# Attention units of a head pair alternate, queries lie by token half, logits are requested by chunks, and inverse row sums are stored as columns

## The chip, the cores and the metric

The kernel runs on one core of one Trainium2 chip. The metric is device time of one execution in microseconds (us); lower is better. Five engines work side by side, each through its own instructions in a fixed order: PE (matrix multiply; its weight loads, "PEld", overlap its matmuls), DVE (vector), ACT (scalar functions), POOL (general, also issues DMAs) and SP (issues most DMAs). Engines wait for each other through semaphores. PE writes to PSUM, of which the kernel uses eight banks of 128 partitions by 512 float32; SBUF holds the operands.

## What is computed

One layer of a decoder for 1024 tokens of width 1024:

```python
h = x @ w_in                       # columns: pool u | q | k | v | forget logits
pool_out = scale * GroupLinear(trailing_mean_w(u) - u)         # w = 2, 4, 8, 16
# attention, 8 heads of 64, causal:
s = q @ k.T * HEAD_DIM**-0.5 + c[t] - c[s]                     # c = cumsum(log sigmoid(f))
attn = softmax(where(s_pos <= t_pos, s, -1e30)) @ v
x = layer_norm(alpha * x + concat(pool_out, attn) @ w_out)
x = layer_norm(alpha * x + relu(x @ w_mlp1)**2 @ w_mlp2)
```

Everything is float32. The kernel splits each operand in a high and a low part and makes three matmuls of one product (`three`, lines 80 to 84).

## The kernel before

The program runs in stages, all of which keep PE busy: values and forget gates and three of the four pool groups (up to about 105 us of the profiled span), attention with the output projection beginning under its end (105 to 345), the rest of the output projection, the first layer norm and both MLP products (a fast 2x2 block scheme), to the end.

**Attention units.** The eight heads form four pairs p = 0 to 3; e = 0, 1 is the head in its pair. A unit (p, e, m) has 256 queries, two tiles of 128 (i = 2m and 2m+1), and the keys up to them, so m = 3 is the heaviest unit and m = 0 the lightest. Line 703 lists the units of pairs 0 to 2 with one head after the other, each falling through m = 3, 2, 1, 0; line 704 lists the last pair with m rising and e inside.

**A unit's two halves.** `att_probs` asks PE for the logits of one query tile in chunks of up to 512 keys (L375, into one of three "s" banks). DVE adds the gate row and finds the running minimum of the negated logits (L380). After the last chunk ACT takes the exponential and its row sum (L382). `att_values` transposes the probabilities on PE (L405, into one of two "pt" banks), splits them (ACT L406, DVE L407) and multiplies with V (L420, into the single "pv" bank); ACT and DVE evacuate that bank (L429, L430) before the next unit's product may begin. `att_values` of one unit runs the generator `att_probs` of the next unit (`ahead`) between its steps: one `yield` per query tile, the first at its first step, the rest at step min(m, (m+1)//2+1).

**Fill.** Between those steps `fillstep` takes pieces of other PE work, three matmuls each: the q and k projection of the next pair (`qk_proj`, L82 to L84 into "mm" banks) in pairs 0 to 2, and in the last pair the last pool group and the output projection of the first two token tiles (`last_fill`). What remains of a projection is run when a pair ends (line 728).

**Row sums.** A head's inverse row sums come from DVE (L443) as columns: [128 tokens, 8 tiles]. `row_scales` turns them on PE (L466, into a "pt" bank), copies them out on ACT into the one buffer `row` (L468) and stores [8, 128] rows to DRAM (`rin_dram`, L469), once per head in pairs 0 to 2 and once per unit in the last pair: 14 times. They are read back, broadcast over partitions, by `attention_part` (L580), which scales the attention output by them (L584) and splits it for the output projection. For the first token tiles the last pair's heads are read by the call named `late` (lines 529 and 544).

**Buffers.** Tags share slots: "A" has 9 (probabilities, their transposes, gate rows), "Q" has 10 (k, q, sums of the pool groups). A gate row of a head (L351) is held from just before its first unit to its last.

**What sets the order.** Each engine's order is fixed at build time by a scheduler that goes through the program's instructions by priority and readiness as it estimates them; on the chip every engine goes through its list in that order, and waits where an operand is late.

Of the kernel before, what the change touches and what calls it, by code (L numbers as in the profile page):

```python
# [14 lines left out]
P = 128  # L15
S = 1024
D = 1024
NT = S // P
# [3 lines left out]
NPAIR = NH // 2  # L22
# [3 lines left out]
CH = 512  # L26
NCH = S // CH
# [9 lines left out]
def trunk(ctx, tc, xT, xn, wuqk, wvf, bf, poolw, pscale, wout, g1, b1, w1, w2, g2, b2, out):  # L37
# [5 lines left out]
    nc = tc.nc  # L43
# [268 lines left out]
    def qk_proj(p, tag=None):  # L312
        if p < NPAIR - 1:
            KS, Q1, Q2 = zip(*([slot("Q", [S]) for _ in range(3)] for _ in range(2)))
            q = {(i, e, c): (Q1, Q2)[i][e][:, c * CH : (c + 1) * CH] for i in range(2) for e in range(2) for c in range(NCH)}
        else:
            KS = [slot("Q", [S]) for _ in range(2)]
            both = {(i, c): slot("Q", [2, CH]) for c in range(NCH) for i in range(2)}
            q = {(i, e, c): both[i, c][:, e] for i in range(2) for e in range(2) for c in range(NCH)}
# [14 lines left out]
        for c in (0, 1) if p == NPAIR - 1 else (1, 0):  # L334
# [18 lines left out]
    def att_probs(p, e, m, prob):  # L353
# [3 lines left out]
        h = 2 * p + e  # L357
# [3 lines left out]
        for i in (2 * m + 1, 2 * m) if falling else (2 * m, 2 * m + 1):  # L361
# [7 lines left out]
            for a in range(0, nk, CH):  # L369
# [11 lines left out]
                top = nm  # L381
            nc.scalar.activation(pt[:, :nk], pt[:, :nk], AF.Exp, bias=nm, scale=-1.0, accum_out=rsum[h][:, i : i + 1])  # L382
            yield

    def att_values(p, e, m, prob, ahead):
# [24 lines left out]
        def multiply(jp, tt):  # L410
# [13 lines left out]
            if jp == m:  # L424
# [10 lines left out]
                if last:  # L435
                    row_scales(h, 2 * m, 2)
                elif m == 0:
                    row_scales(h, 0, NT)

        if p == NPAIR - 1 or m == 0:  # L440
            ri = small([P, NT], "ri", bufs=3)
            i, n = (2 * m, 2) if p == NPAIR - 1 else (0, NT)
            nc.vector.reciprocal(ri[:, :n], rsum[h][:, i : i + n])  # L443
            inverse[h, i] = ri

        for jp in range(m + 1):
            left.append((multiply, jp, turned(jp)))
            if jp == 0:
                fill["last"] = fill["sub"]
                next(ahead, None)  # L450
            if jp == min(m, (m + 1) // 2 + 1):
                run(ahead)
# [3 lines left out]
    left, inverse = [], {}  # L456
# [5 lines left out]

    def row_scales(h, i, n):
        ri = inverse.pop((h, i))
        tp = bank("pt")
        nc.tensor.transpose(tp[0:n, 0:P], ri[:, :n], ident)  # L466
        row = small([NT, P], "row")
        nc.scalar.copy(row[0:n], tp[0:n, 0:P])  # L468
        nc.sync.dma_start(rin_dram[h, i * P : (i + n) * P].rearrange("(i q) -> i q", q=P), row[0:n])  # L469
# [233 lines left out]
    order = [(p, e, m) for p in range(NPAIR - 1) for e in range(2) for m in (3, 2, 1, 0)]  # L703
# [631 lines left out]
```

## Time and profile before

| | |
|---|---|
| median of 3 runs | 1028.21 us (1027.87 to 1028.32) |
| the profiled execution | 1028.26 us, its span 1026.5 us |
| granted PE clock over the span | 0.997 |
| PE busy | 1013.1 us, 99% |
| DVE, ACT, POOL busy | 754.4 us, 513.3 us, 153.6 us |

A span is the time from the first to the last instruction of the program; 1.8 us of the execution lie around it. Matmuls overlap in the profile: one of 512 columns is shown with 0.39 us, but the next may start 0.23 us after it. So "PE busy 99%" hides short waits, and starts that are further apart than usual show them. In "engine line waited for" rows the numbers are the sum in us, the times, and the longest.

### The profile page before, as it was taken

To read this page: it belongs to the slowest core of one execution; us is meant where nothing else is said; L and a number is where in the kernel's file an instruction comes from. 1 tells how busy PE (TensorE), PEld (TensorE's weight loads), DVE (VectorE), ACT (ScalarE), POOL (GpSimd) and SP (SyncE) were. 2 spreads that over 40 slices of the span, in tenths; PEclk is the share of its full clock that TensorE was granted. 3 is DMA by queue.
4 is the path that set the end of the run, shared out by engine and by line. 5 is a ranking of instruction groups with operands and counts; after the bars stand their busy time and mean duration, and the time that the engine had idled before them with its cause. 6 is when DMAs were issued, how large, how long until landed. Compare 5 with 4: busy or idle time off the path is not lost.

```text
span 1026.5 us, 14095 instructions
## 1 busy us (share of the span) xinstructions
PE 1013.1 (99%) x4976; PEld 843.8 (82%) x4976; DVE 754.4 (73%) x1303; ACT 513.3 (50%) x825; POOL 153.6 (15%) x269
## 2 busy tenths in 40 slices
PE   9999999999999999999999999999999999999996
PEld 9988888888788888888888888888888888888884
DVE  6576677777868798989888787798866565565547
ACT  5423665666755333678667667669521121221152
POOL 0200111111110032112221221220000000000057
PEclk9999999999999999999999999999999999999998
DMA  9702211111682633259676675665999888878753
GB/s 354 285 28 88 97 52 53 34 48 52 205 290 91 188 141 103 82 185 362 235 273 236 241 275 222 251 260 191 350 309 289 298 265 264 289 237 274 231 179 123
DMA packets 113399, 206.17 MB, mean 201 GB/s; under 512 B 9576, under 2 KB 77608, under 8 KB 113328
## 3 DMA queue, kind: packets, MB, share of 16 engines
q1 hardware_dynamic: 94176, 136.97, 40.7%
q0 software_dynamic: 18720, 67.64, 17.0%
q8 instruction: 39, 0.64, 0.2%
q10 hardware_dynamic: 432, 0.66, 0.2%
q14 instruction: 32, 0.26, 0.1%
HBM read 132.29 MB, written 72.94 MB: 200 GB/s over the span
## 4 chain that ended last, share of the span: by engine, by line
PE 58%; DVE 2%; issue 0%; ACT 0%; DVEq 0%
PE s L1136 17%; PE s L796 11%; PE pv L1136 9%; PE mm L796 7%; PE pt L796 7%; PE pv L796 4%; PE pt L1136 2%; PE mm L1136 2%; DVE B L71 0%; DVE bns L639 0%; DVE A L664 0%; DVE pt L661 0%; DVE pt L1153 0%; DVE A L870 0%; DVE pv L1153 0%
## 5 line engine op out<-in xcount | busy, mean ns | idle before, releaser
L71 ACT CAST B<-S 128x1024 fp32r<-128x1024 f32 (+1 forms) x78 | 67.6, 880 | 162.9 <-DMA S<-in_w_dram 85.0
L796 PE MATMUL s<-B,Q 128*128 128x512 f32 x492 | 116.4, 389 | 0.2 <-ACT B L71 0.2
L796 PEld LDWEIGHTS s<-B,Q 128*128 128x128 f32 x492 | 92.3, 188 | 19.7 <-ACT B L71 0.6
L71 DVE TENSOR_TENSOR B<-S,B 128x1024 fp32r<-128x1024 f32 (+1 forms) x78 | 78.0, 1008 | 37.7 <-ACT B L71 37.6
L1136 PE MATMUL s<-B,Q 128*128 128x512 f32 x402 | 98.5, 390 | 0.0
L1136 PEld LDWEIGHTS s<-B,Q 128*128 128x128 f32 x402 | 75.5, 188 | 16.5
L71 ACT CAST Q<-S 128x1024 fp32r<-128x1024 f32 (+2 forms) x54 | 55.7, 1031 | 63.6 <-PE s L796 17.0
L921 POOL DMA_DIRECT2D hid_dram<-A x90 | 48.1, 538 | 218.1 <-ACT A L918 171.5
L1136 PE MATMUL s<-B,A 128*128 128x512 f32 x321 | 80.3, 394 | 0.0
L71 DVE TENSOR_TENSOR Q<-S,Q 128x1024 fp32r<-128x1024 f32 (+2 forms) x54 | 65.5, 1213 | 12.8 <-ACT Q L71 12.6
L796 PE MATMUL pt<-B,Q 128*128 128x512 f32 x312 | 74.6, 389 | 0.0
L1136 PEld LDWEIGHTS s<-B,A 128*128 128x128 f32 x321 | 60.4, 188 | 13.9
L796 PE MATMUL mm<-B,Q 128*128 128x512 f32 x300 | 71.6, 389 | 0.0
L382 ACT ACTIVATE A<-A,nm 128x1024 f32<-128x1024 f32 (+7 forms) x64 | 49.7, 777 | 42.0 <-DVE nm L380 41.9
L407 DVE TENSOR_TENSOR A<-pt,A 128x512 fp32r<-128x512 f32 (+1 forms) x80 | 50.1, 633 | 25.1 <-ACT A L406 24.3
L796 PEld LDWEIGHTS pt<-B,Q 128*128 128x128 f32 x312 | 58.5, 188 | 12.1
L796 PEld LDWEIGHTS mm<-B,Q 128*128 128x128 f32 x300 | 56.3, 188 | 11.7
L919 DVE TENSOR_TENSOR A<-A,A 128x1024 f32<-128x1024 f32 x45 | 53.6, 1218 | 0.0
L406 ACT CAST A<-pt 128x512 fp32r<-128x512 f32 (+1 forms) x80 | 42.4, 541 | 22.2 <-PE pt L405 21.6
L375 PE MATMUL s<-Q,Q 128*128 128x512 f32 (+2 forms) x192 | 52.2, 368 | 1.3 <-DVE nm L380 1.3
L420 PE MATMUL pv<-A,B 128*128 128x256 f32 x320 | 53.1, 289 | 0.2 <-DVE U L430 0.2
L420 PEld LDWEIGHTS pv<-A,B 128*128 128x128 f32 x320 | 45.8, 189 | 6.4 <-DVE U L430 3.2
(432 smaller groups left out, 2290.1 us busy)
## 6 DMA issues: line engine op xcount, KB each, us to landing
hid_dram<-A POOLq DMA_DIRECT2D x105, 512.0 KB, 3.8
S<-in_w_dram SPq DMA_DIRECT2D x62, 512.0 KB, 4.4
Q<-hid_dram SPq DMA_DIRECT2D x98, 256.0 KB, 5.3
A<-hid_dram SPq DMA_DIRECT2D x82, 256.0 KB, 5.3
S<-in_wuqk_dram SPq DMA_DIRECT2D x12, 512.0 KB, 4.7
wo_dram<-Q POOLq DMA_DIRECT2D x10, 512.0 KB, 4.3
B<-wo_dram SPq DMA_DIRECT2D x10, 512.0 KB, 6.8
Q<-hid_dram SPq DMA_DIRECT2D x39, 128.0 KB, 3.2
```

The lines of the kernel that those rows point to most:

```text
L71: return nc.scalar.copy(hi, src).ins, nc.vector.tensor_tensor(lo, src, hi.bitcast(F32), ALU.subtract).ins
L375: nc.tensor.matmul(sp, rows, KS[:, a:b], start=n == 0, stop=n == 1 and not diag)
L382: nc.scalar.activation(pt[:, :nk], pt[:, :nk], AF.Exp, bias=nm, scale=-1.0, accum_out=rsum[h][:, i : i + 1])
L406: nc.scalar.copy(tt[:, 0, ev], tp[:, ev])
L407: fill["sub"] = nc.vector.tensor_tensor(tt[:, 1, ev], tp[:, ev], tt[:, 0, ev].bitcast(F32), ALU.subtract).ins
L420: nc.tensor.matmul(ov, V[j][:, h].rearrange("p s d -> p (s d)"), tt[:, s, a:b], start=(j == 0 and s == 0), stop=(j == 2 * m + 1 and s == 1),)
L796: nc.tensor.matmul(dst, b[x][:, k], A[a][y][:, k], start=first and k == 0 and i == 0, stop=k == H - 1 and i == 2, skip_group_check=not first,)
L919: nc.vector.tensor_tensor(x, x, hi.bitcast(F32), ALU.subtract)
L921: nc.gpsimd.dma_start(hid_dram[self.u, :, i, AT[name] : AT[name] + 2 * CH], part.rearrange("p q n t -> p (q n t)"))
L1136: nc.tensor.matmul(dst, h[:, p_], w[q_], start=first and u == self.us[0] and j == 0, stop=u == self.us[-1] and j == 2, skip_group_check=no ...
```

## The change

- Pairs 0 to 2 list their units with the two heads alternating: (3, e=0), (3, e=1), (2, e=0) and so on. The last pair's list is as it was.
- `qk_proj` allocates q of every pair by token half, both heads in one slot, as the last pair did already; six slots for a pair as before. Pairs 0 to 2 make the second token half first.
- `att_probs` yields after each chunk of logits, not only after a query tile, and `att_values` asks for one piece at each of its steps but the last, and for the rest at the last.
- `row_scales` is gone. The inverse row sums are stored as the columns they are, straight from DVE's output, by one DMA when a head's (or last pair's unit's) probabilities are done: [128, 8] or [128, 2] single elements of 4 bytes to places of stride 1 over the partitions. This stands at the start of `att_values` and no longer behind its last multiply.

```diff
     def qk_proj(p, tag=None):
-        if p < NPAIR - 1:
-            KS, Q1, Q2 = zip(*([slot("Q", [S]) for _ in range(3)] for _ in range(2)))
-            q = {(i, e, c): (Q1, Q2)[i][e][:, c * CH : (c + 1) * CH] for i in range(2) for e in range(2) for c in range(NCH)}
-        else:
-            KS = [slot("Q", [S]) for _ in range(2)]
-            both = {(i, c): slot("Q", [2, CH]) for c in range(NCH) for i in range(2)}
-            q = {(i, e, c): both[i, c][:, e] for i in range(2) for e in range(2) for c in range(NCH)}
+        halves = (0, 1) if p == NPAIR - 1 else (1, 0)
+        KS = [slot("Q", [S]) for _ in range(2)]
+        both = {(i, c): slot("Q", [2, CH]) for c in halves for i in range(2)}
+        q = {(i, e, c): both[i, c][:, e] for i in range(2) for e in range(2) for c in range(NCH)}
...
                 top = nm
+                if b < nk:
+                    yield
             nc.scalar.activation(pt[:, :nk], pt[:, :nk], AF.Exp, bias=nm, scale=-1.0, accum_out=rsum[h][:, i : i + 1])
...
-                if last:
-                    row_scales(h, 2 * m, 2)
-                elif m == 0:
-                    row_scales(h, 0, NT)
 
         if p == NPAIR - 1 or m == 0:
-            ri = small([P, NT], "ri", bufs=3)
             i, n = (2 * m, 2) if p == NPAIR - 1 else (0, NT)
+            ri = small([P, NT], "ri", bufs=4)
             nc.vector.reciprocal(ri[:, :n], rsum[h][:, i : i + n])
-            inverse[h, i] = ri
+            nc.sync.dma_start(rin_dram[h, i * P : (i + n) * P].rearrange("(i q) -> q i", q=P), ri[:, :n])
 
         for jp in range(m + 1):
             left.append((multiply, jp, turned(jp)))
             if jp == 0:
                 fill["last"] = fill["sub"]
+            if jp < m:
                 next(ahead, None)
-            if jp == min(m, (m + 1) // 2 + 1):
+            else:
                 run(ahead)
...
-    order = [(p, e, m) for p in range(NPAIR - 1) for e in range(2) for m in (3, 2, 1, 0)]
+    order = [(p, e, m) for p in range(NPAIR - 1) for m in (3, 2, 1, 0) for e in range(2)]
     order += [(NPAIR - 1, e, m) for m in range(4) for e in range(2)]
```

How the order of the engines changes, at three places. A row names the line, the operation, out<-in and the shape.

**PE, the heaviest unit (m = 3) of the second head of pair 1.** Q_1201 (before) and Q_1202 (changed) hold its k as s<-Q; mm is fill. Before:

```order
L375 MATMUL s_2058<-Q_1201,Q_1202 128x512
L375 MATMUL s_2058<-Q_1201,Q_1203 128x512
L375 MATMUL s_2063<-Q_1201,Q_1202 128x512
L375 MATMUL s_2063<-Q_1201,Q_1203 128x512
L375 MATMUL s_2071<-Q_1201,Q_1202 128x512
L375 MATMUL s_2071<-Q_1201,Q_1203 128x512
L82 MATMUL mm_2042<-B_390,B_2039 128x512
L83 MATMUL mm_2042<-B_390,B_2039 128x512
L84 MATMUL mm_2042<-B_390,B_2039 128x512
L420 MATMUL pv_1216<-A_1984,B_417 128x256
L375 MATMUL s_2076<-Q_1201,Q_1202 128x384
L375 MATMUL s_2076<-Q_1201,Q_1203 128x384
```

Changed (L372 is what L375 was):

```order
L372 MATMUL s_1809<-Q_1202,Q_1203 128x512
L372 MATMUL s_1809<-Q_1202,Q_1204 128x512
L83 MATMUL mm_1744<-B_172,B_1741 128x512
L372 MATMUL s_1833<-Q_1202,Q_1203 128x512
L372 MATMUL s_1833<-Q_1202,Q_1204 128x512
L84 MATMUL mm_1744<-B_172,B_1741 128x512
L82 MATMUL mm_1744<-B_172,B_1741 128x512
L372 MATMUL s_1860<-Q_1202,Q_1203 128x512
L372 MATMUL s_1860<-Q_1202,Q_1204 128x512
L83 MATMUL mm_1744<-B_172,B_1741 128x512
L84 MATMUL mm_1744<-B_172,B_1741 128x512
L82 MATMUL mm_1744<-B_187,B_1741 128x512
```

Three banks were filled in one go and the fourth chunk followed four matmuls later; now the chunks stand apart, and the fourth one (not shown) comes after two groups of transposes. The first unit of pairs 1 and 2 still asks for three banks in one go.

**PE, unit (0, 0, 2), from the last logits to its transposes.** Before, from its last logits on (s_1282):

```order
L375 MATMUL s_1282<-Q_975,Q_977 128x256
L82 MATMUL mm_1209<-B_172,B_1206 128x512
L405 MATMUL pt_1252<-ident_63,A_1152 128x128
L405 MATMUL pt_1252<-ident_63,A_1139 128x128
L405 MATMUL pt_1252<-ident_63,A_1152 128x128
L405 MATMUL pt_1252<-ident_63,A_1139 128x128
L420 MATMUL pv_1216<-A_1218,B_417 128x256 x4
L83 MATMUL mm_1209<-B_172,B_1206 128x512
L405 MATMUL pt_1267<-ident_63,A_1139 128x128
L405 MATMUL pt_1267<-ident_63,A_1152 128x128
L405 MATMUL pt_1267<-ident_63,A_1139 128x128
L84 MATMUL mm_1209<-B_172,B_1206 128x512
```

Changed, the same (last logits s_1386, first transpose pt_1405):

```order
L372 MATMUL s_1386<-Q_975,Q_978 128x256
L82 MATMUL mm_1323<-B_397,B_1209 128x512
L83 MATMUL mm_1323<-B_397,B_1209 128x512
L84 MATMUL mm_1323<-B_397,B_1209 128x512
L419 MATMUL pv_1219<-A_1332,B_430 128x256 x4
L82 MATMUL mm_1323<-B_404,B_1209 128x512
L83 MATMUL mm_1323<-B_404,B_1209 128x512
L84 MATMUL mm_1323<-B_404,B_1209 128x512
L82 MATMUL mm_1323<-B_404,B_1209 128x512
L83 MATMUL mm_1323<-B_404,B_1209 128x512
L84 MATMUL mm_1323<-B_404,B_1209 128x512
L404 MATMUL pt_1405<-ident_63,A_1365 128x128
```

Before, eleven more rows stand between the last one shown and the unit's own transposes; now these come at the end of the piece.

**SP, in the last pair, up to the loads that `attention_part` makes for the first three pairs (S<-mix, S<-rin).** Before:

```order
L432 DMA mix_dram<-U_3041 64x256
L561 DMA B_3215<-wo_dram 128x1024
L469 DMA rin_dram<-row_3120 8x128
L561 DMA B_3216<-wo_dram 128x1024
L432 DMA mix_dram<-U_3114 64x256
L561 DMA B_3215<-wo_dram 128x1024
L469 DMA rin_dram<-row_3164 2x128
L577 DMA S_3183<-mix_dram 128x768
L580 DMA S_3184<-rin_dram 64x3x256 x2
```

Changed:

```order
L439 DMA rin_dram<-ri_2986 128x2x1
L549 DMA B_3048<-wo_dram 128x1024
L431 DMA mix_dram<-U_3023 64x256
L549 DMA B_3184<-wo_dram 128x1024
L439 DMA rin_dram<-ri_3060 128x2x1
L549 DMA B_3185<-wo_dram 128x1024
L431 DMA mix_dram<-U_3097 64x256
L439 DMA rin_dram<-ri_3104 128x2x1
L549 DMA B_3184<-wo_dram 128x1024
L565 DMA S_3157<-mix_dram 128x768
L568 DMA S_3158<-rin_dram 64x3x256 x2
```

The store of head 5 (128x8x1) has moved further up, ahead of the first of these wo loads, and three stores of the last pair's units stand before the loads where one row store stood. From the second part of the output projection on (the last 1010 rows of PE) every engine's order is what it was, but for buffer numbers.

More of the change, by code (lines that the diff above doesn't have):

```diff
@@ L333, in qk_proj @@
         sc = HD ** -0.5
-        for c in (0, 1) if p == NPAIR - 1 else (1, 0):
+        for c in halves:
             qp = bank(tag)
@@ L454, in att_values @@
             values(2)
-    left, inverse = [], {}
+    left = []
     def values(n):
@@ L461, in values @@
             step(jp, tt)
[L463 to L469, printed above, removed]
     g0 = qk_proj(0)
```

## The prediction

> **What bounds the kernel now.** I read the page first, then the chain of work that ended last, then a table of windows by stage, then what PE's weight loads waited for between 105 and 345 us, then the timeline at single waits. Page, part 1 and the chain by engine:
>
> ```profile
> PE 1013.1 (99%) x4976; PEld 843.8 (82%) x4976; DVE 754.4 (73%) x1303; ACT 513.3 (50%) x825; POOL 153.6 (15%) x269
> PE 58%; DVE 2%; issue 0%; ACT 0%; DVEq 0%
> ```
>
> PE is the bound, and the chain names almost nothing else. The windows (us, then busy time of PE, PEld, DVE, ACT, POOL with counts, PE's granted clock, DMA share, GB/s):
>
> ```profile
> 105.00:262.00 157.00, 155.61 (x912) 130.73 (x911) 117.72 (x290) 101.81 (x217) 26.58 (x72) 1.00 0.18 56
> 262.00:345.00 83.00, 82.23 (x461) 66.77 (x459) 61.32 (x140) 48.15 (x99) 8.50 (x18) 1.00 0.62 198
> 345.00:1014.00 669.00, 668.82 (x2958) 550.18 (x2957) 500.26 (x715) 317.90 (x429) 104.24 (x139) 1.00 0.69 238
> ```
>
> From 345 us on PE idles for 0.2 of 669 us and its order is unchanged, so what attention gains or loses arrives at the end at full value. The granted clock is 1.00 in all three, so no term comes from it. In attention the 2.2 us that PE shows as idle are not all that it loses, because a matmul is drawn longer than the distance to the next start. The weight loads show the waits better (sum in us, times, longest):
>
> ```profile
> PEld s L375 <- DVE nm L380: 4.6, 10, 0.9
> PEld pv L420 <- DVE U L430: 3.2, 10, 0.6
> PEld pt L405 <- ACT A L382: 2.5, 9, 0.4
> PEld pt L405 <- ACT row L468: 2.3, 6, 0.6
> ...
> PEld pt L466 <- DVE A L407: 1.4, 6, 0.2
> ```
>
> Logits wait for a free "s" bank, values for the "pv" bank's evacuation, transposes for the exponential or for the row sums' copy. These five rows hold 14.0 us, of which PE feels a part. With the turned sums' own time this bounds the gain.
>
> **Term 1, row sums leave PE: -1.5 us.** Fourteen transposes and fourteen ACT copies go:
>
> ```profile
> L466 PE MATMUL pt<-ident,ri 128*2 128x128 f32 (+1 forms) x14 | 3.8, 272 | 0.0
> ```
>
> What one takes is its share of the starts, not 272 ns. In the timeline (start, length):
>
> ```profile
> 188.11 0.39 PE L83 MATMUL mm<-B,B 128*128 128x512 f32 x1
> 188.34 0.39 PE L84 MATMUL mm<-B,B 128*128 128x512 f32 x1
> ```
>
> and at a transpose of row sums
>
> ```profile
> 317.09 0.40 PE L84 MATMUL mm<-B,Q 128*128 128x512 f32 x1
> 317.40 0.27 PE L466 MATMUL pt<-ident,ri 128*2 128x128 f32 x1
> 317.42 0.71 PE L375 MATMUL s<-Q,Q 128*128 128x512 f32 x2
> 318.13 0.55 PE L405 MATMUL pt<-ident,A 128*128 128x128 f32 x3
> ```
>
> Full matmuls start 0.23 apart. From 317.09 to 317.42 it is 0.33 with the transpose between, so 0.10 to 0.11 each, and 14 x 0.11 = 1.5 us. The bound above is the 3.8 us of the group. The copies were off the path in themselves: ACT is busy 150 of 240 us here. What takes their place is one DMA issue on SP, of which more below, and the reciprocal, which DVE makes before and after.
>
> **Term 2, waits for the row copy: -1.1 us.** The one buffer `row` is not what PE waits for; the "pt" bank that holds the turned sums is, until ACT has copied it. Where it shows:
>
> ```profile
> 223.07 0.49 PE L375 MATMUL s<-Q,Q 128*128 128x512 f32 x1
> 223.70 0.44 PE L405 MATMUL pt<-ident,A 128*128 128x128 f32 x2
> ```
>
> ```profile
> 275.47 0.33 PE L375 MATMUL s<-Q,Q 128*128 128x384 f32 x1
> 276.07 0.66 PE L405 MATMUL pt<-ident,A 128*128 128x128 f32 x4 [0.27 <-ACT row L468]
> ```
>
> 0.63 - 0.23 = 0.40; 0.60 - 0.17 (three quarters of 0.23 for 384 columns) = 0.43; at 317.42, 0.71 - 0.46 = 0.25: 1.1 us. The other three of the six I take as hidden. Between nothing, if the transposes would have waited for something else at the same moment, and 2.3 + 1.4 = 3.7, all that the two weight-side rows hold, I take what is seen.
>
> **Term 3, logits no longer pile up at a head's start: -1.0 us.** A light unit's values with a heavy unit's four chunks is where the three "s" banks run full. Heads 3 and 5 (the second of pairs 1 and 2) and heads 2 and 4 (the first):
>
> ```profile
> 188.56 0.28 PE L420 MATMUL pv<-A,B 128*128 128x256 f32 x1
> 189.17 0.62 PE L375 MATMUL s<-Q,Q 128*128 128x384 f32 x2 [0.33 <-DVE nm L380]
> 189.63 0.52 PE L420 MATMUL pv<-A,B 128*128 128x256 f32 x3
> ```
>
> ```profile
> 240.19 0.40 PE L83 MATMUL mm<-B,B 128*128 128x512 f32 x1
> 240.75 0.61 PE L375 MATMUL s<-Q,Q 128*128 128x384 f32 x2 [0.17 <-DVE nm L380]
> ```
>
> ```profile
> 215.14 0.39 PE L83 MATMUL mm<-B,B 128*128 128x512 f32 x1
> 216.02 0.62 PE L375 MATMUL s<-Q,Q 128*128 128x384 f32 x2 [0.49 <-DVE nm L380]
> ```
>
> and DVE at the first of them:
>
> ```profile
> 187.69 0.69 DVE L331 TENSOR_TENSOR Q<-mm,Q 64x512 fp32r<-64x512 f32 x1
> 188.41 0.69 DVE L380 CUSTOM_DVE_ANT_0 A<-s,A 128x512 f32<-128x512 f32 x1
> ```
>
> At 188 DVE was still evacuating the k projection (L331) when the three chunks lay ready, and PE's fourth chunk started 0.61 after a 256-column matmul, which alone takes 0.12 ((0.52 - 0.28) / 2 in the row of three): 0.49 lost; at 240, 0.56 - 0.23 = 0.33. With alternating heads these two units follow a unit of equal size, and the order spreads their chunks over fill and transposes, so 0.8 goes, and I add 0.2 for smaller places. The places at 215 (0.65) and at head 2 remain: a pair still begins behind its predecessor's lightest unit, and one step then asks for everything. The bounds are 0 and 1.5, all three.
>
> **Term 4, transposes closer behind their logits: +0.5 us.** In unit (0, 0, 2) the changed order has nine full matmuls and four of 256 columns between the last logits and the transposes: 9 x 0.23 + 4 x 0.12 = 2.5 us, about half of before. The bare chain there is a reduction of 128 columns, its reading, an exponential of 640, its reading:
>
> ```profile
> L380 DVE CUSTOM_DVE_ANT_0 A<-s,A,nm 128x128 f32<-128x128 f32 x8 | 2.8, 347 | 0.4 <-DVE nm L380 0.2
> L380 DVE DVE_READ_ACCUMULATOR2_ANT nm<- 128x1 f32 x96 | 7.9, 82 | 0.0
> L382 ACT ACTIVATE A<-A,nm 128x640 f32<-128x640 f32 x8 | 6.6, 831 | 13.3 <-DVE nm L380 13.3
> L382 ACT ACTIVATION_READ_ACCUMULATOR A<-A,nm 128x1 f32 x64 | 12.0, 187 | 0.0
> ```
>
> 1.45 us, so 1.1 us are left for one ACT or DVE instruction ahead of it, not for three. The logits are late by being asked for later, so PE work that used to stand behind them is now ahead. If such waits double, weight loads wait 2.5 us more, and PE feels about half of it (of 2.3 in term 2 it felt 1.1): +1.2. If the order fits as before, 0. I take +0.5. Next in line behind late transposes are ACT's and DVE's splits and then L420; "pt" banks gain, since no turned sums pass through them.
>
> **Term 5, the output projection's late operand: +0.2 us.** In the last pair PE already waits for `late`:
>
> ```profile
> 304.74 0.50 PE L82 MATMUL mm<-B,Q 128*128 128x512 f32 x1 [0.23 <-ACT Q L71]
> ```
>
> ```profile
> q1 hardware_dynamic: 2908, 7.33, 79.4%
> ...
> S<-rin_dram SPq DMA_DIRECT2D x2, 64.0 KB, 6.7
> ```
>
> Its load took 6.7 us to land in a queue that, between 276 and 304 us, fills 79% of the 16 DMA engines. PE will be there sooner by what the last pair gains before it (four or five transposes and one 0.43 wait, 0.9 us); if the loads don't come sooner too, that is lost here: 0 to 0.9. They are freed by the same PE work, so I take 0.2.
>
> The new stores also write 4-byte pieces: 6 x 1024 + 8 x 256 = 8192 packets. On this trace a packet of SP's queue takes 71 ns on average (page, part 3), and 122 ns in the full window (0.794 x 16 x 28 us / 2908):
>
> ```profile
> q1 hardware_dynamic: 94176, 136.97, 40.7%
> ```
>
> Those packets carry 1.5 to 2.5 KB each, so this bounds a 4-byte one from above: a store of 1024 takes at most 4.5 us, of 256 at most 2 us in the full window. Pairs 0 to 2 read their sums a pair later, and SP's queue has room (window at 18%), so the six cost nothing while the DMA share is low. The stores now start at the unit's first step, earlier than the rows did.
>
> The Trainium skill, "DMA: Bandwidth & Descriptors", section "Rules for kernel authors", speaks against this edit: a last dimension that is strided is lowered to one descriptor per element, and should be made contiguous. By the same page's floor of about 10.5 ns per packet a store of 1024 would take some 0.7 us, an estimate; no row here shows a 4-byte store.
>
> In SP's queue a store waits for the reciprocal and holds up what stands behind it: the gate row of the next pair's second head, and in the last pair wo loads. The reciprocal is ready when the unit's transposes may start, while the row it replaces waited for a multiply behind them, so nothing there is later. The mask additions on POOL (15% busy) keep their number, and q six slots to a pair; both gate rows of a pair now hold an "A" slot through it, which can only show in terms 3 and 4.
>
> **Sum:** -1.5 - 1.1 - 1.0 + 0.5 + 0.2 = -2.9 us on the profiled execution of 1028.26, so 1025.4; the median of the runs is 0.05 below, so **1025.3 us**, 0.28% faster. Its own range is 1023.9 to 1026.1 (a term or two at a bound).
>
> **Rivals.** *Waits only move* (chance 0.22): a different bank or chain is last at the same spots, as at L420, whose 3.2 us nothing here removes and which has more short units back to back now. Then only term 1 stays: 1026.7, no measurable change. *More than the sum* (0.13): the even load also takes the remaining L375 stalls (0.7 more) and half of L420's felt part (0.8 of 1.6), with terms 4 and 5 at 0: 5.1 us, 1023.1. For it: DVE is busy 118 of 157 us, so queues and not capacity make its waits. Against: DVE's evacuations stand where they stood. *Transposes arrive before their exponentials* (0.08, slower): the second tile's chunks, asked for late, make PE wait at L405 in every unit. Twenty-four units in pairs 0 to 2 at 0.25 us, the size of the visible row wait, are 6 us, with 3.6 of gains left: 1030.6. It decides from 0.15 us per unit. Against: today's waits there, 2.5 us in 9 places, come with equally tight light units. *Column stores fill the DMA queue* (0.05): three stores stand before the loads of term 5; at 2 us each `late` slips by 6 us, and with 3.1 gained the kernel ends at 1031. This is what the skill's rule would do at its worst; it decides from 1 us per store. Against: their size. The forecast keeps 0.52.
>
> A measurement of this kernel tells about 0.2%, 2.06 us, from no change. Faster by more: most of the forecast and the larger gain, 0.62. Slower by more: 0.11. Within: 0.27. The range reaches from 1021.8 (the larger gain with term 2 at half its bound, 2.4) to 1028.8 (terms 2 and 3 at nothing, 4 and 5 at their upper ends), and leaves out the two slow rivals and a little of the larger gain.
>
> **What would show it.** Right: no L466 or L468 rows, no "PEld pt L405 <- ACT row" wait, the L375 wait row near 2.5 to 3 us instead of 4.6, with its long ones at the starts of pairs 1 and 2 only; L405 <- ACT A L382 no higher than 4; the stage from 105 us to the unchanged order shorter by about 3 us. Wrong: L405 <- ACT A L382 beyond 6 us, L420 <- DVE U L430 up by what L375 lost, or a PE wait on L71 over 1 us at the out-projection's late operand with stores that take over 2 us.

## The result: 3.65% slower

The changed kernel takes 1066.3 us (median of 4 runs, 1064.8 to 1067.5) against 1028.3 us for the kernel before: a ratio of 1.0365, with a 95% interval of 1.0345 to 1.0385. Forecast were 1025.3 us. The profiled execution took 1064.8 us, its span is 1063.0.

The page of the changed kernel, parts 1, 2 and 4: busy times, PE's granted clock by slice, and the chain by engine.

```profile
PE 1020.0 (96%) x4962; PEld 851.5 (80%) x4962; DVE 755.9 (71%) x1303; ACT 512.0 (48%) x811; POOL 158.4 (15%) x269
PEclk9999999989889999999999999999999999999998
PE 56%; DVE 2%; issue 0%; ACT 0%; DVEq 0%
```

PE has 14 instructions fewer, as planned, and yet is busy 6.9 us longer, at a clock that is below 9 tenths in three slices, all of them in attention. The windows of the changed kernel (columns as before, PE busy first, the last three PE's clock, DMA share and GB/s):

```profile
105.00:262.00 157.00, 146.47 (x832) 123.12 (x831) 108.58 (x261) 93.14 (x191) 27.69 (x63) 0.97 0.28 47
262.00:345.00 83.00, 62.86 (x333) 51.07 (x331) 44.25 (x114) 37.13 (x85) 9.54 (x21) 0.91 0.74 156
380.00:1049.00 669.00, 668.78 (x2966) 551.48 (x2965) 501.14 (x715) 319.60 (x431) 102.68 (x138) 1.00 0.69 239
```

The last row is the part whose order is unchanged, taken 35 us later than in the kernel before and as full as there (668.78 of 669 us). So the loss is made between 105 and 380 us. What weight loads and matmuls waited for between 105 and 400 us (sum, times, longest):

```profile
PEld pt L404 <- ACT A L381: 19.8, 14, 7.9
PEld s L372 <- DVE nm L377: 12.8, 9, 5.9
PEld pv L419 <- DVE U L429: 8.4, 10, 4.8
PEld mm L82 <- DVE B L609: 1.7, 1, 1.7
```

```profile
PE pt L404 <- ACT A L381: 15.5, 6, 7.8
PE s L372 <- DVE nm L377: 9.8, 3, 5.4
PE pv L419 <- DVE U L429: 4.7, 2, 4.4
PE mm L82 <- DVE B L609: 1.2, 1, 1.2
```

The matmul rows add up to 31.2 us, of which six single waits make nearly all; before it was 2.0. They name the exponential, the running minimum and an evacuation, but ACT and DVE are no busier than before. They are 5.4, 4.2, 6.6, 7.8, 1.2 and 4.4 us long, in order of time. What those engines waited for is on the timeline around the first and the fourth (start, length, engine, line, [idle before <- releaser]):

```profile
171.41 0.81 POOL L363 TENSOR_TENSOR A<-A,maskb 128x128 f32<-128x128 f32 x2 [8.68 <-DMA A<-ncf_dram]
172.25 0.62 DVE L377 CUSTOM_DVE_ANT_0 A<-s,A,nm 128x384 f32<-128x384 f32 x1 [5.65 <-POOL A L363]
172.93 0.79 PE L372 MATMUL s<-Q,Q 128*128 128x512 f32 x1 [5.44 <-DVE nm L377]
```

```profile
303.84 0.36 ACT L428 COPY U<-pv 64x256 f32<-64x256 f32 x1 [7.05 <-DMA mix_dram<-U]
304.99 0.48 PE L404 MATMUL pt<-ident,A 128*128 128x128 f32 x1 [7.76 <-ACT A L381]
```

At 172.93 PE waits for DVE, DVE for POOL's mask addition, POOL for a gate row. At 304.99 PE waits for ACT, and ACT for the buffer U, which a store of attention output has not left yet. All are transfers. SP's issues ahead of the first:

```profile
156.62 0.38 SPq L439 DMA_DIRECT2D rin_dram<-ri  x1
157.37 0.45 SPq L431 DMA_DIRECT2D mix_dram<-U  x1
157.96 0.49 SPq L348 DMA_DIRECT2D A<-ncf_dram  x1
160.20 0.37 SPq L439 DMA_DIRECT2D rin_dram<-ri  x1
```

The late gate row is the one issued at 157.96, 1.3 us behind a column store with one store of attention output between them; it landed 13.3 us later. Over attention (150 to 420 us; transfers, size of one, median us from issue to landing):

```profile
A<-ncf_dram SPq DMA_DIRECT2D x6, 512.0 KB, 11.2
rin_dram<-ri SPq DMA_DIRECT2D x8, 1.0 KB, 12.4
rin_dram<-ri SPq DMA_DIRECT2D x6, 4.0 KB, 12.8
```

A store of 1024 elements, and just so one of 256, takes over 12 us, and the gate rows take 11.2. The third long wait is at another load: ACT waits 7.4 us for a weight block of the output projection, and PE 6.6 us for ACT.

**Half clock.** Each of the five waits of over 4 us brings the granted clock down to 0.50, from late in the wait until 3 to 6 us behind it; the windows right behind the two waits shown:

```profile
172.90:176.10 3.20, 3.17 (x10) 2.58 (x11) 1.72 (x3) 1.13 (x2) 1.34 (x1) 0.50 0.09 20
304.90:309.20 4.30, 4.21 (x14) 3.52 (x15) 1.43 (x4) 2.37 (x7) 0.00 (x0) 0.50 0.97 55
```

The Trainium skill, "TensorE: Matmul & The Clock Gate", Part 1, says that PE falls to half its clock after an idle window of about 3.4 us; this trace agrees: 4.25 us and more were followed by 0.50, the wait of 1.2 us was not. In the runs below, waits of 3.2 to 3.8 us were followed by it too, and one of 2.6 us (column stores alone) was not. The account closes with it. The spans differ by 36.5 us, and the change without its stores gains about 3 (experiment below), so some 40 have to be found. 29 are longer waits of PE. Behind the five waits PE runs at half clock for 3.2, 5.5, 5.0, 4.3 and 4.5 us, 22.5 in all, and half of that, 11, is lost.

### The profile page after: what moved, and what is told of

It is laid out like the page before. It is cut to its first block, busy times and chain, and to the rows that moved or that the text cites. A ratio compares the mean times of both kernels' runs of the same rounds, so it can differ in the third digit from the quotient of the medians.

```text
span 1063.0 us, 14053 instructions
## 1 busy us (share of the span) xinstructions
PE 1020.0 (96%) x4962; PEld 851.5 (80%) x4962; DVE 755.9 (71%) x1303; ACT 512.0 (48%) x811; POOL 158.4 (15%) x269
## 4 chain that ended last, share of the span: by engine, by line
PE 56%; DVE 2%; issue 0%; ACT 0%; DVEq 0%
PE s L1124 16%; PE s L784 10%; PE pv L1124 8%; PE mm L784 6%; PE pt L784 6%; PE pv L784 4%; PE pt L1124 2%; PE mm L1124 2%; DVE B L71 0%; DVE bns L627 0%; DVE A L652 0%; DVE pt L649 0%; DVE pt L1141 0%; DVE A L858 0%; DVE pv L1141 0%
## 5 line engine op out<-in xcount | busy, mean ns | idle before, releaser
L71 ACT CAST B<-S 128x1024 fp32r<-128x1024 f32 (+1 forms) x78 | 67.7, 880 | 169.6 <-DMA S<-in_w_dram 96.9
L71 DVE TENSOR_TENSOR B<-S,B 128x1024 fp32r<-128x1024 f32 (+1 forms) x78 | 77.9, 1008 | 38.3 <-ACT B L71 38.1
L71 ACT CAST Q<-S 128x1024 fp32r<-128x1024 f32 (+2 forms) x54 | 55.7, 1031 | 65.7 <-PE s L784 15.8
L71 DVE TENSOR_TENSOR Q<-S,Q 128x1024 fp32r<-128x1024 f32 (+2 forms) x54 | 65.4, 1212 | 12.7 <-ACT Q L71 12.6
L1124 PEld LDWEIGHTS s<-B,A 128*128 128x128 f32 x321 | 60.3, 188 | 13.3
L784 PEld LDWEIGHTS mm<-B,Q 128*128 128x128 f32 x300 | 56.3, 188 | 11.7
L372 PE MATMUL s<-Q,Q 128*128 128x512 f32 (+2 forms) x192 | 55.8, 383 | 9.9 <-DVE nm L377 9.8
L405 ACT CAST A<-pt 128x512 fp32r<-128x512 f32 (+1 forms) x80 | 43.1, 542 | 43.4 <-PE pt L404 39.8
L404 PE MATMUL pt<-ident,A 128*128 128x128 f32 x288 | 48.5, 286 | 15.6 <-ACT A L381 15.5
L419 PEld LDWEIGHTS pv<-A,B 128*128 128x128 f32 x320 | 48.9, 196 | 12.9 <-DVE U L429 8.4
```

The source lines that it names most:

```text
L71: return nc.scalar.copy(hi, src).ins, nc.vector.tensor_tensor(lo, src, hi.bitcast(F32), ALU.subtract).ins
L372: nc.tensor.matmul(sp, rows, KS[:, a:b], start=n == 0, stop=n == 1 and not diag)
L404: fill["turn"] = nc.tensor.transpose(tp[:, col : col + P], prob[ii][:, j * P : (j + 1) * P], ident).ins
L405: nc.scalar.copy(tt[:, 0, ev], tp[:, ev])
L419: nc.tensor.matmul(ov, V[j][:, h].rearrange("p s d -> p (s d)"), tt[:, s, a:b], start=(j == 0 and s == 0), stop=(j == 2 * m + 1 and s == 1),)
L784: nc.tensor.matmul(dst, b[x][:, k], A[a][y][:, k], start=first and k == 0 and i == 0, stop=k == H - 1 and i == 2, skip_group_check=not first,)
```

## The experiments

Theory A: the column stores are the cause. Theory B: the new order is, with transposes and logits too close to what they need. In the diffs a sign is against the changed kernel, or against the kernel before where that is said.

### Stores back to rows

```diff
+                if last:
+                    row_scales(h, 2 * m, 2)
+                elif m == 0:
+                    row_scales(h, 0, NT)
...
-            nc.sync.dma_start(rin_dram[h, i * P : (i + n) * P].rearrange("(i q) -> q i", q=P), ri[:, :n])
+            inverse[h, i] = ri
```

(`row_scales` itself comes back as it was.)

> The changed kernel with one part undone: the row sums are turned on PE, copied by ACT and stored as rows [8, 128] or [2, 128] again, behind the last multiply of the unit as before; alternation, q by token half and chunkwise requests stay. Theory A (the column stores: their 1024 or 256 single elements each hold SP's queue for about 10 us, loads behind them land late, and PE then runs at half its clock for some us): without them all of the 38 us go, 1025 to 1030 us, and no wait of PE on L71, L609 or on a gate row is over 1 us. Theory B (the new order itself: transposes and logits asked for too tightly): most of the loss stays, 1045 us or more. If both are at work, something between, 1032 to 1045.

Measured: 1028.07 us, ratio 0.9997 (0.9988 to 1.0006). All of the loss is gone. The longest wait of a matmul is 1.1 us. The weight loads:

```profile
PEld pt L404 <- ACT A L381: 6.4, 14, 1.5
PEld s L372 <- DVE nm L377: 2.7, 8, 0.5
PEld pt L404 <- ACT row L468: 2.3, 6, 0.6
```

Theory B falls as the cause of the loss. The order does have an effect, seen here as the first row at 6.4 where it was 2.5, and the second at 2.7 where it was 4.6; below it is taken apart.

### Column stores alone

Against the kernel before:

```diff
-                if last:
-                    row_scales(h, 2 * m, 2)
-                elif m == 0:
-                    row_scales(h, 0, NT)
...
-            inverse[h, i] = ri
+            nc.sync.dma_start(rin_dram[h, i * P : (i + n) * P].rearrange("(i q) -> q i", q=P), ri[:, :n])
```

> The kernel before with the column stores alone: heads in their old order, logits by tile, no turning of row sums on PE, 14 stores of single elements. Theory A: slower by 8 to 35 us, 1036 to 1063; the starts of pairs 1 and 2 stall less than in the changed kernel, because the gate row of the next head then stands at another place of SP's queue, while the last pair's stalls (loads of wo and of the row sums, stores of mix) stay. Theory B: the stores cost next to nothing, 1025 to 1028.

Measured: 1044.0 us, ratio 1.0157 (1.0143 to 1.0170). The same 14 stores with landings nearly as long (the large ones 10.7 us), but 16 us and not 38:

```profile
A<-ncf_dram SPq DMA_DIRECT2D x6, 512.0 KB, 3.7
rin_dram<-ri SPq DMA_DIRECT2D x8, 1.0 KB, 12.6
```

Gate rows land in 3.7 us here: with heads one after the other the next head's gate row is issued 4 to 7 us ahead of the store. So the stores take about as long in both, and what differs is what stands behind them: the alternation put the gate row of a pair's second head 1.2 to 1.3 us behind one. The combination cost more than its parts.

### Gate rows ahead of the stores

```diff
+            if n % 8 == 7:
+                gate_row(2 * order[n + 1][0] + 1)
```

> The changed kernel with one load moved: the gate row of a pair's second head is requested together with the first one's, ahead of both column stores of the pair before, so that it cannot stand behind them. The stores stay. If the stalls at the starts of pairs come from that gate row landing behind a store: the waits of 5.4, 4.2 and 6.7 us at the three starts go or shrink below 2 us, with the stretches of half clock after them, 1066 - 16 - 7 = 1043 us (1040 to 1054); the last pair's stalls stay. If the logits themselves came late for another reason: 1060 us or more.

Measured: 1050.0 us, ratio 1.0212 (1.0198 to 1.0226). The first of the two stages is whole again, and the wait for logits back at its level without column stores:

```profile
105.00:262.00 157.00, 155.88 (x916) 131.51 (x915) 120.01 (x292) 102.67 (x215) 31.26 (x73) 1.00 0.22 59
PEld s L372 <- DVE nm L377: 2.5, 8, 0.5
```

Sixteen of the 38 us came from late gate rows. The waits of 5.4 and 4.2 us at the starts of pairs 1 and 2 are gone; the third, expected to go as well, stays at 6.5 us, for it was not a gate row that came late there. The rest is the last pair, whose stores of U and loads stay behind column stores: PE waits there 6.5, 3.4, 3.7 and 4.5 us.

### The stores from another queue

```diff
-            nc.sync.dma_start(rin_dram[h, i * P : (i + n) * P].rearrange("(i q) -> q i", q=P), ri[:, :n])
+            nc.scalar.dma_start(rin_dram[h, i * P : (i + n) * P].rearrange("(i q) -> q i", q=P), ri[:, :n])
```

> The changed kernel with the column stores issued by ACT and not by SP; all loads, mix stores and gate rows stay in SP's queue. Theory A1 (a store holds up only what stands behind it in its own queue): gate rows and wo loads land on time again, 1025 to 1034 us, with the wait for the row sums themselves left at `late`. Theory A2 (the single elements occupy the 16 DMA engines, so that every queue is slowed): most of the loss stays, 1050 us or more. Theory B: no change from 1066.

Measured: 1069.8 us, ratio 1.0415 (1.0390 to 1.0439): no help, rather 3.5 us more. So it is not that SP's queue is served in order. The DMA view for 159.5 to 167.5 us, after the 1024 elements had left ACT's queue (packets; then packets, MB and the share of 16 engines of SP's queue):

```profile
DMA packets 126, 0.52 MB, mean 65 GB/s; under 512 B 0, under 2 KB 0, under 8 KB 126
q1 hardware_dynamic: 126, 0.52, 117.1%
```

None of these packets belongs to a column store, and each takes 1.171 x 16 x 8 / 126 = 1.2 us. The Trainium skill, "DMA: Bandwidth & Descriptors", section "Issuing engines are not separate DMA queues", says that DMAs of all issuing engines run on the same 16 engines; the run agrees.

The same view of the changed kernel shows what the price is not. While the elements themselves are taken, 157.5 to 158.5 us, and then 161 to 167:

```profile
DMA packets 983, 0.09 MB, mean 90 GB/s; under 512 B 959, under 2 KB 963, under 8 KB 983
q1 hardware_dynamic: 983, 0.09, 72.8%
```

```profile
DMA packets 64, 0.26 MB, mean 44 GB/s; under 512 B 0, under 2 KB 0, under 8 KB 64
q1 hardware_dynamic: 64, 0.26, 120.6%
```

and the kernel before, loading a gate row from 157 to 159.5 us:

```profile
DMA packets 134, 0.48 MB, mean 193 GB/s; under 512 B 16, under 2 KB 16, under 8 KB 134
q1 hardware_dynamic: 134, 0.48, 55.6%
```

A 4-byte packet takes at most 0.728 x 16 / 983 us = 12 ns of one engine's time (24 of the 983 are larger). A packet of the loads behind takes 1.206 x 16 x 6 / 64 = 1.8 us, where it took 0.556 x 16 x 2.5 / 134 = 0.17 before. The stores are cheap in their own packets; the transfers that follow pay.

### The same bytes in one piece per partition

```diff
-            nc.sync.dma_start(rin_dram[h, i * P : (i + n) * P].rearrange("(i q) -> q i", q=P), ri[:, :n])
+            nc.sync.dma_start(rin_dram[h, i * P : (i + n) * P].rearrange("(q i) -> q i", q=P), ri[:, :n])
```

> The changed kernel with the same 14 stores at the same places of SP's queue and of the same bytes, but each partition writes its 8 (or 2) sums as one contiguous piece of 32 (or 8) bytes: 128 descriptors a store and not 1024 or 256. It leaves out the transposition of the sums: they lie in DRAM by partition and not by tile, so that the attention output is scaled by sums of other tokens; all other work is what it was. Theory A, with the number of descriptors as the cause: a store of 128 lands in 2 to 3.5 us, and the time is 1024 to 1029 us. If the cause were the stores' place in the queue, or their early start, whatever their form, or if Theory B held: 1060 us or more.

Measured: 1028.8 us, ratio 1.0005 (0.9995 to 1.0015). Same place, same start, same bytes, and the loss is gone. The landings from 150 to 420 us:

```profile
rin_dram<-ri SPq DMA_DIRECT2D x8, 1.0 KB, 6.3
rin_dram<-ri SPq DMA_DIRECT2D x6, 4.0 KB, 2.1
A<-ncf_dram SPq DMA_DIRECT2D x6, 512.0 KB, 3.6
```

So neither the place nor the early start is the cause, but the form. Both kinds of store have 128 pieces, and the small ones, pieces of 8 bytes, are the slower ones; but they stand in the last pair, where the DMA share is 0.66 (0.18 from 150 to 262 us), so this does not tell whether the number of pieces decides or their size.

### What a store costs by its form

First, ten stores of copied values added to the kernel before, with nothing tied to them:

> The price of a store by its form: the kernel before, plus ten stores of a copied tile to places that nobody reads, two of each form, during pairs 0 to 2: 128, 256, 512 and 1024 single elements of 4 bytes ([128, 1], [128, 2], [128, 4], [128, 8], stored as columns), and 1024 elements as 128 pieces of 32 bytes. If a column store's time goes by its number of single elements (the 10 to 11 us of 1024 say about 9 ns each over a fixed 2 us, 0.15 us for each of an engine's 64): 3, 4, 6 and 11 us, and 2 to 3 us for the 128 pieces of 32 bytes, like the 128 elements. If it goes by bytes: all near 2 us. If it is a fixed price of a strided store: all four columns near 10 us.

Measured: 1028.2 us in its one run, as the kernel before. Nothing waited for these stores, so no landing shows, and none of the three laws is told apart. It does show, in one run, that column stores cost nothing by themselves if nothing behind them is urgent. So the next run put a load behind each, and had its landing waited for (POOL copies eight columns of it):

```diff
+                nc.gpsimd.tensor_copy(cp, pt[:, :NT])
+                if n:
+                    to = to[:, 0] if form == "lines" else to[: n * P]
+                    nc.sync.dma_start(to.rearrange("(q i) -> q i" if form == "piece" else "(i q) -> q i", q=P), cp[:, :n])
...
+                nc.sync.dma_start(probe, src)
+                nc.gpsimd.tensor_copy(cp, probe[:, :NT])
```

> The kernel before with eleven probes in pairs 0 to 2: a store of copied values to a place that nobody reads, and right behind it in SP's queue a load of 128 x 4 KB whose landing is waited for. Forms ahead of the load: none; 128, 256, 512 and 1024 single elements; 1024 elements as 128 pieces of 32 bytes; 1024 single elements each in a 64-byte line of its own; 1024 single elements with a load from another DRAM array (a weight) behind. Theory A, sharpened by the ten stores that stood alone and cost nothing: single-element writes are taken from the queue in about 1 us but hold back the loads that follow, by 9 to 10 us for 1024. Then the load lands after 2 to 4 us with none or pieces ahead, after some 4, 5, 7 and 12 us with 128 to 1024 elements. If it is because neighbours of one line are written one by one, the elements in lines of their own land the load in 3 to 6 us; if every write of 4 bytes has its price, in 12 us again. If it is the place in DRAM, the load from the other array lands in 3 to 5 us; if all loads are held, in 12.

The rows of a probe: the load's issue on SP, POOL's copy of what it loaded (count, duration, first and last start in us).

```profile
L400 SPq DMA_DIRECT2D pone<-ncf_dram x1: 372/372/372, 192.6 to 192.6; - x1
L401 POOL COPY cp<-pone x1: 189/189/189, 204.3 to 204.3; 128x8 f32<-128x8 f32 x1
```

```profile
L400 SPq DMA_DIRECT2D plines<-ncf_dram x2: 513/522/531, 171.4 to 291.9; - x2
L401 POOL COPY cp<-plines x2: 189/189/189, 179.2 to 297.9; 128x8 f32<-128x8 f32 x2
```

From issue to copy, which bounds the landing from above, worked out from such rows (to within 0.1, as their times are rounded):

| ahead of the load | us |
|---|---|
| nothing | 4.0 and 4.7 |
| 128 pieces of 32 bytes | 4.0 |
| 128 single elements | 11.7 |
| 256 single elements | 10.6 |
| 512 single elements | 13.2 |
| 1024 single elements | 15.2 and 14.8 |
| 1024, load from another DRAM array | 12.6 |
| 1024, each in a 64-byte line of its own | 7.8 and 6.0 |

The expected 4, 5, 7, 12 are refuted: 128 elements hold a load almost as long as 1024. This fits the stores of 256 in the last pair, which took what the large ones did. The other array is held as well. What frees the load is distance between the elements, to about half of the time here. (This run's own time, 1090 us, is long: POOL waits for the probes, and PE waits up to 10.8 us between them.) The last run varies that distance.

> What of a column store holds the loads behind it. The probes gave a load behind 128 neighbouring single elements 11.7 us, behind 1024 of them 15, behind 1024 elements at a distance of 64 bytes 6 to 8, with none 4 to 5: so not the number of elements. Here the same probes with the distance of neighbouring elements changed: 128 elements at 4 (twice), 32, 64 and 512 bytes, 1024 at 4, 16, 32, 64 and 512 bytes, and one with none. If elements that share a 64-byte piece of DRAM are written one after the other: near 11 us at 4 bytes, clearly less at 16 and 32 (4 and 2 to a piece instead of 16), and 4.5 to 8 from 64 on, where more distance changes nothing. If it were larger pieces (512 bytes): 64 bytes lies between and 512 is the first to be free. If the element count had its own price: 1024 at 512 bytes stays 6 us or more, and 128 at 512 bytes is at 4 to 5.

```profile
L399 SPq DMA_DIRECT2D pline<-ncf_dram x1: 372/372/372, 185.0 to 185.0; - x1
L400 POOL COPY cp<-pline x1: 190/190/190, 189.0 to 189.0; 128x8 f32<-128x8 f32 x1
```

```profile
L399 SPq DMA_DIRECT2D ptight<-ncf_dram x2: 377/380/382, 130.9 to 282.2; - x2
L400 POOL COPY cp<-ptight x2: 189/189/189, 141.7 to 291.1; 128x8 f32<-128x8 f32 x2
```

| distance, bytes | 4 | 16 | 32 | 64 | 512 | no store |
|---|---|---|---|---|---|---|
| 128 elements, us | 10.8 and 8.9 | | 6.0 | 4.0 | 3.7 | 3.4 |
| 1024 elements, us | 10.7 | 8.4 | 5.0 | 6.7 | 5.1 | |

With 128 elements it falls as the distance grows and is at the level of no store from 64 bytes on, where more distance brings nothing. With 1024 it falls from 10.7 over 8.4 to 5 to 7, and 512 bytes are not better than 32; some 2 us of their own remain. This fits writes that share a small piece of DRAM and are made one by one, while later loads wait. How large the piece is stays open between 32 and 64 bytes: there are single probes only, and they point both ways (6.0 and 4.0 us with 128 elements, 5.0 and 6.7 with 1024). No run shows where in the memory or on the way to it this happens. The Trainium skill, "DMA: Bandwidth & Descriptors", section "Specifications", gives 512 bytes as the transfer size below which a DMA does a read-modify-write. The sizes here are 4, 8 and 32 bytes and the 512 of the row stores, and 32 already cost nothing visible; the distances show no bend at 512.

### What the rest of the change is worth

No stores at all:

```diff
+    nc.sync.dma_start(rin_dram[:, :].rearrange("h (a b) -> (h a) b", b=HD), ident[:, :HD])
...
-            nc.sync.dma_start(rin_dram[h, i * P : (i + n) * P].rearrange("(i q) -> q i", q=P), ri[:, :n])
```

> The changed kernel without any of the 14 column stores. It leaves out the storing of the sums: the place in DRAM is filled once, before attention, with a constant, and attention is scaled by that; the reciprocals, the loads of the sums and all else stay. It shows what the change would be worth if its stores cost nothing. By the terms of the prediction with the stores at nothing (row sums leave PE, waits for the row copy, logits no longer piled up, transposes closer): about 1025.3 us, 0.3% under the kernel before. By the rival that waits only move: 1026.7 us. If the turned sums were hidden anyway: 1028, no change.

Measured: 1024.96 us, ratio 0.9968 (0.9956 to 0.9981). The terms other than the stores add up as forecast, and the 1026.7 of *waits only move* lies outside the interval. To split them, the alternation alone, against the kernel before:

```diff
-    order = [(p, e, m) for p in range(NPAIR - 1) for e in range(2) for m in (3, 2, 1, 0)]
+    order = [(p, e, m) for p in range(NPAIR - 1) for m in (3, 2, 1, 0) for e in range(2)]
```

(with q by token half)

> The kernel before with the alternation of heads and q by token half alone: logits by tile and row sums turned on PE as before. By term 3 of the prediction (logits no longer pile up at a head's start, -0.8 of -1.0 from the order of the units): 1027.3 us. If waits only move: 1028.3. If the transposes come too early because of the order and not of the chunks: 1029 us or more, with the weight loads' wait for the exponential near the 6.4 us that the changed order with rows shows; if it is the chunks, that wait stays near the 2.5 us of before.

Measured: 1030.0 us, ratio 1.0017 (1.0008 to 1.0026): slightly slower.

```profile
PEld pt L402 <- ACT A L379: 7.7, 18, 1.5
PEld s L372 <- DVE nm L377: 2.2, 7, 0.5
```

And the chunkwise requests alone, against the kernel before too:

```diff
+                if b < nk:
+                    yield
...
-            if jp == min(m, (m + 1) // 2 + 1):
+            else:
                 run(ahead)
```

> The kernel before with the chunkwise requests alone: heads one after the other, row sums turned on PE as before. Measured so far: the alternation alone is 1030.0 us, alternation and chunks with rows 1028.1, the kernel before 1028.4. If the chunks are what gains (logits spread over the steps) and the alternation what costs: 1026.5 to 1027.5 us, with the weight loads' wait for a logits bank near 2.7 us instead of 4.6. If the two only help each other (the chunks mend what the alternation does): 1028 to 1029, no change.

Measured: 1027.3 us, ratio 0.9989 (0.9980 to 0.9998), a gain just outside the measurement's doubt.

```profile
PEld s L375 <- DVE nm L380: 4.6, 9, 0.9
PEld pt L407 <- ACT A L384: 1.8, 5, 0.8
```

It is the alternation that removes the wait for logits banks (4.6 to 2.2) and pays with waits for the exponential (2.5 to 7.7). The chunks leave the logits row at 4.6, against the expectation of 2.7; what falls with them are the transposes' rows (for the exponential 2.5 to 1.8, for the row copy 2.3 to 1.1).

### A version that beats both

Rows again, but both heads' sums of a pair turned by one transpose, in the changed order:

```diff
+            nc.vector.reciprocal(inverse[p, i][:, e], rsum[h][:, i : i + n])
...
+                if e and (last or m == 0):
+                    row_scales(p, *((2 * m, 2) if last else (0, NT)))
...
+        nc.tensor.transpose(tp[0 : 2 * n, 0:P], ri.rearrange("p e i -> p (e i)"), ident)
+        nc.scalar.copy(row[0 : 2 * n], tp[0 : 2 * n, 0:P])
```

> A version that may beat both: the changed order, rows instead of columns, but the sums of a pair's two heads, which end one after the other now, are turned by one transpose of 16 (or 4) columns, copied once and stored by two row stores: 7 transposes and 7 copies instead of 14. If turning a head's sums costs PE 0.11 us by itself and about 0.2 with the wait for the copy: 1.0 to 1.4 us under the kernel with rows and the changed order, 1026.7 to 1027.1. If turned sums are hidden anyway: 1028, no change. The second theory would add that the row of a pair's first head is ready a unit later, which could delay the last load of the sums: up to 1030.

Measured: 1025.53 us, ratio 0.9973 (0.9963 to 0.9984), faster than before and within 0.6 us of the version without any stores. Halving the transposes gained 2.5 us over rows with the changed order, twice what was expected; the weight loads' wait for the row copy went nearly whole with it (it was 2.3):

```profile
PEld pt L404 <- ACT row L466: 0.3, 1, 0.3
```

The same with heads one after the other:

> The chunkwise requests and the paired turning without the alternation: heads one after the other as before, the first head's inverse sums wait for the second's, both are turned by one transpose and stored as rows. The measured parts: chunks alone 1027.3 us; pairing took 2.5 us off the changed order with rows (1028.1 to 1025.5); alternation alone cost 1.5. If these add: 1024.7 us (1024 to 1025.5), faster than every version so far or the same as the paired one with alternation. If the pairing gained only because the alternation lets both heads end together: 1026 to 1027.

Measured: 1025.9 us, ratio 0.9974 (0.9962 to 0.9986), the same as the paired version with alternation. Whether the parts add is open: the sum of 1024.7 lies just within the interval. By the medians pairing gave 1.4 here and not 2.5, which fits the row wait that the chunks alone had already brought from 2.3 to 1.1.

## Why the prediction was wrong, step by step

**The step that failed is term 5, the column stores.** It took an average of SP's packets, 71 ns, as a bound from above for a 4-byte packet, so "a store of 1024 takes at most 4.5 us, of 256 at most 2 us". The packet's own time was well inside that bound (12 ns); the inference from it to the store's time was wrong. Measured were 12.8 and 12.4 us, and the transfers behind were held with them: a load's packet took 1.8 us and not 0.17. "So the six cost nothing while the DMA share is low" assumed that a quiet queue hides a store; at the starts of pairs 1 and 2 the share was low, and there the alternation put an urgent load behind it. The text had named that load ("the gate row of the next pair's second head") and let it go with "nothing there is later", which looked at when the store is issued and not at when it lets go. And with the long waits half clock came on top, some 11 us, which no term held.

**The rival of the column stores** had the right cause and sign, and was given 0.05. Its price, 2 us a store, was the upper end of the same wrong bound, and its argument against, "their size", missed that such small pieces are dear when they lie side by side. Its place was wrong: at `late` PE shows no wait in the changed kernel; the smallest of the six waits (1.2 us) comes soon after, behind a load of token rows. The gate rows, the weight block and the buffer U were not in it. The Trainium skill's rule against strided last dimensions was cited and right in its advice. Its 10.5 ns per packet was misused: the Trainium skill, "DMA: Bandwidth & Descriptors", section "Bandwidth", gives it for a whole load, 0.67 us for 64 packets, and the prediction divided it by the 16 engines once more. Undivided it makes 10.8 us for 1024 packets, an estimate near the 12.8 measured; but the runs do not show its rule, since 256 elements took 12.4 us and 128 held a load almost as long as 1024.

**Terms 1 and 2, row sums leave PE:** the sum was right. Forecast -2.6 us; from rows to no stores in the changed order it is 1028.07 - 1024.96 = 3.1. The split is not shown: halving the transposes gained 2.5, where half of the two terms is 1.3.

**Terms 3 and 4:** the sum fits, but can't be told from nothing, and its parts were not right. Forecast with the load part of term 5 -0.3; rows in the changed order against before, -0.4 (-1.2 to 0.6). Term 3's mechanism held, the row at 2.7 us where "2.5 to 3" was named, through the alternation as said. Term 4 put the doubling at 2.5 us and on chunks asked for late; the wait rose by 3.9 and comes from the alternation, which alone costs 1.5 us, while the chunks gain 1.1. So of *waits only move* this much is true: alternation trades one wait for another.

**Signs.** "L405 <- ACT A L382 beyond 6 us" was to mean that the forecast is wrong; without the stores it is 6.3 and the time is as forecast. It was set too close. The wait on L71 at the late operand, the sign that was to show dear stores, does not appear in the changed kernel, although its stores take over 12 us. *Transposes arrive before their exponentials* has its wait, but not its price: PE feels 2 us of it in all, not 6.

## What to carry to other kernels

Price a store by what is held behind it, not by its own packets or bytes: in the probes 128 neighbouring 4-byte elements were enough to hold the load behind them for 4 to 8 us, and stores of 256 and 1024 held loads from SP's queue and from ACT's. One contiguous piece of 32 bytes per partition, or a transpose on PE before a store of rows, avoids it (the piece leaves the sums in another order in DRAM, which what reads them would have to undo). Before a reordering puts an urgent load behind a store, look at which of the two is issued first; and count a PE wait of over 3 us with the half clock that followed every such wait looked at here. A transposed copy that cannot be dropped may be halved: turning two heads' sums at once got nearly all that leaving the turning out would have.

## What the runs showed of the hardware, unexpected

- A burst of 4-byte writes to neighbouring places in DRAM is taken from the queue at no more than 12 ns of an engine's time a packet, and the loads behind it then need 1.2 to 1.8 us per 4 KB packet for some 9 us.
- The time depends on the distance of the elements more than on their number: 128 at 4 bytes 8.9 to 11.7 us, 1024 at 4 bytes 10.7 to 15.2, 128 at 64 bytes 4.0, 1024 at 64 bytes 6.0 to 7.8, at 512 bytes 5.1, no store 3.4 to 4.7.
- In such a stretch the DMA view shows a full share (over 100%) at 44 GB/s: a busy share says that transfers are open, not that bytes move.
